# Every fourth split of a weight tile has its lower part subtracted by GpSimd in place of VectorE

## The chip, the core and the metric

The kernel runs on one core of one Trainium2 chip. The metric is the device time of one execution in microseconds, as the median of repeated executions. The core's engines work side by side, each with its own in-order queue: TensorE (PE in the rows, its weight loads PEld) multiplies matrices, VectorE (DVE) and ScalarE (ACT) work elementwise, GpSimd (POOL) here clears a few tiles and issues some DMAs, SyncE (SP) issues the others.

## The reference

One decoder block over 512 tokens of 1024 channels, in float32. The input is normed; its products with `w_in` feed a gated short convolution and a differential attention of 8 heads; both are gated, added and put back into the residual. A cross-attention of 4 heads over 256 memory positions follows. Last, a layer of 16384 single-neuron experts: each of 8 heads scores 2 x 128 keys, keeps the best 16 of each half, then the best 16 of their sums, softmaxes these, and the chosen rows of `peer_u` and `peer_v` give

```python
act = gelu(einsum('td,thkd->thk', hc, peer_u[experts]))
out = einsum('thk,thkd->td', g * act, peer_v[experts])
```

The sum with the residual is normed once more.

## The kernel before

Activations lie channel by token: a product has a weight tile of 1024 x 128 (eight blocks of 128 x 128) on one side and up to 512 tokens on the other.

**The split.** Every float32 product runs as three passes in TensorE's faster float32r format, over exact two-part splits: high x high, high x low, low x high. ScalarE copies the tile `raw` to `hi`, which rounds it; the lower part is what is left, `lo = raw - hi`. `split` (line 97) does both; its second line is an instruction of VectorE over 128 x 1024 float32. `weight` (line 106) loads a tile on SyncE's queue and splits it; `product` (line 114) then issues 8 x 3 matmuls, of which the third already reads `lo`. The tags `raw`, `hi` and `lo` have three buffers each, so a tile is loaded and split while the two before it are multiplied, and `hi` of a new tile waits until the product three tiles back has been done.

**The stages in order of time.** The memory's keys and values (12 tiles by `weight`). The eight heads and the convolution (48 tiles); then the gated outputs, the mix, the cross-attention and its output (56 tiles). The choice of keys, `keys_scores` and `keys_pairs`: 16 tiles of `w_pq`, and VectorE's searches for the best 16. The gates, `gates` (line 823): for blocks of 24 tokens, one-hot rows by ScalarE and VectorE, multiplied by TensorE. During keys and gates TensorE also runs products of `uT`, 96 of 128 tiles by `stage_u` (line 687), to fill its waits. The experts' loop, `experts` (line 713): for each of 128 blocks j it loads a tile of `peer_v`, splits it with the same tags, multiplies the activations by the gates (line 739, VectorE), splits these (`tr` by ScalarE and `e` by VectorE) and adds 18 matmuls of 512 columns to six banks (line 750). For j from 85 to 116 each step also runs one of the other 32 `uT` tiles.

**GpSimd's queue.** In the heads it clears masked blocks of the attention weights (lines 304 and 305), whose buffers come free with the matmuls of line 312. At the start it writes the table of the relative bias to DRAM (line 219). The first 128 tokens take their experts by gathered rows, `gathered` (line 774): one indirect DMA per row (line 818), 256 in all, issued by GpSimd after VectorE has copied the row's index (line 798) and the row's buffer is free (VectorE's lines 801 and 812, whose weight comes by the copy of line 808).

**What sets the order.** The program is written stage by stage, but the order of each engine's queue is laid out by a planner, which simulates the program with its own costs (`schedule_with_timeline_sim`, line 933) and puts the instructions of all engines in the order of that simulated time. On the chip each engine keeps to that order and waits at the head of its queue.

Of the kernel before, what the change touches and what calls it, by code (L numbers as in the profile page):

```python
"""Hybrid block on one core: gated short conv + differential attention, memory cross-attention, PEER.

Activations are channel-major ([channel, token]) up to the expert layer. Every float32 product runs
as three float32r passes over exact two-part splits (hi*hi + hi*lo + lo*hi). The expert layer takes
the first 128 tokens by gathering the rows they chose, and the other 384 against all experts on the
tensor engine, with the gates laid out densely.
"""
# [34 lines left out]
# the order of the work  # L42
EARLY = 5  # convolution channels kept beside the chunks
LAG = 1  # heads before the first convolution channels
SOON = 5  # memory weights loaded ahead of the input
PROLOGUE = 96  # blocks of experts activated before the first is summed up
BY_HEAD = 5  # of them, by each head's choice of experts
BY_BLOCK = 3  # and by each block of tokens' gates
FILL = 4  # and at the end of the gates
AHEAD = 11  # blocks activated ahead of the sum after that  # L50
NA = 3  # one-hot rows of four that ScalarE makes
MM = 1  # gate banks taken from the products
X_HEAD = 4  # gathered rows by two heads' choice
X_BLOCK = 3  # and by each block of tokens' gates
XW = 3  # rows in a step with an activation, to one in a step without
LAST = 2  # steps without rows at the end
LAST_J = 2  # blocks summed up token block by token block at the end
# [4 lines left out]
class Block:  # L62
    # tag: (pool, slots)
# [13 lines left out]
    def __init__(self, nc, tc, pools, psum, dram, a):  # L77
        self.nc, self.tc, self.pools, self.psum, self.dram, self.a = nc, tc, pools, psum, dram, a
        self.count = 0

# [10 lines left out]
    def rows(self, name):  # L91
        """a vector on every partition"""
        src = self.a[name]
        return bass.AP(tensor=src.tensor, offset=src.offset, ap=[[0, P], [1, D]])

# [1 line left out]
    def split(self, hi, lo, src):  # L97
        self.nc.scalar.activation(hi, src, AF.Copy)  # L98
        self.nc.vector.tensor_tensor(out=lo, in0=src, in1=hi.bitcast(F32), op=ALU.subtract)  # L99
# [6 lines left out]
    def weight(self, dram_ap):  # L106
        raw = self.t("raw", [P, KC, P])
        self.nc.sync.dma_start(out=raw, in_=dram_ap)
        hi = self.t("hi", [P, KC, P], F32R)
        lo = self.t("lo", [P, KC, P], F32R)  # L110
        self.split(hi, lo, raw)
        return hi, lo

    def product(self, out, w, x):
        """out[c, t] = sum over d of w[d, c] x[d, t]"""
# [22 lines left out]
    def roots(self, out, acc, n, inv, eps, log=False, bank="tr"):  # L138
        """out[t, i] = 1 / sqrt(inv * sum of squares + eps) of token 128 i + t; acc holds sums by partition"""
# [7 lines left out]
    def inverse_root(self, out, ss, inv, eps, log=False):  # L147
        """1 / sqrt(ss * inv + eps). By log: exp(-log / 2), and a Newton step, where ScalarE holds that table; else three
        Newton steps from the exponent halved in the bits"""
# [16 lines left out]
    def spread(self, r, n, bank="tr"):  # L166
        """the tokens' values along the free dim, on every partition (in PSUM)"""
# [24 lines left out]
    def parameters(self):  # L192
        nc, a, m = self.nc, self.a, self.misc
        nc.vector.tensor_scalar(out=self.g_sub, in0=self.small[:, 56:57], scalar1=1.0 - LAM_INIT, scalar2=None, op0=ALU.mult)
        # lambda = exp(q1.k1) - exp(q2.k2) + init, the same on every partition
# [9 lines left out]
        # relative bias by distance, reversed: entry e stands for distance 511 - e  # L205
# [36 lines left out]
    def diff_head(self, h, x):  # L242
# [4 lines left out]
        # each component's 64 channels on both halves of the partitions: queries as (hi, lo), keys as (hi, hi)  # L247
# [21 lines left out]
        for pair in range(2):  # L269
            # weights of two query blocks, two key blocks to a tile  # L270
            ahi = [self.t("aw", [P, 2, 2 * P], F32R) for _ in range(pair + 1)]
            alo = [self.t("aw", [P, 2, 2 * P], F32R) for _ in range(pair + 1)]
            for qi in range(2):
# [24 lines left out]
                for b in range(pair + 1):  # L298
# [3 lines left out]
                    if m == 1:  # L302
                        # this key block is all in the future of the pair's first query block
# [32 lines left out]
    def gated(self, sg, w_out, y, gate, x):  # L336
        """sigmoid(gate projection) * (y @ w_out)"""
# [7 lines left out]
    def add_and_scale(self, w, y, res, g):  # L345
        """res += y @ w, in place; returns the split of res * g, and the sums of squares by partition"""
# [19 lines left out]
    def memory(self):  # L366
        """keys and values of the cross-attention, to DRAM: the products need no norm, which scales the positions"""
# [5 lines left out]
        # some weights ahead of the input, which the norm needs as a whole  # L373
# [50 lines left out]
    def mem_keys(self):  # L424
        """channel-major: [channel, position] by chunk"""
        out = []
# [7 lines left out]
    def mem_values(self):  # L434
        """token-major: [position, part, position block, channel] by chunk"""
# [62 lines left out]
    def keys_scores(self, h, x, yk, xk):  # L498
        """the best 16 keys of each half, for the dense and for the gathered tokens"""
# [15 lines left out]
    def keys_pairs(self, n, vals, idx, ei, ej, ez):  # L515
        """the best 16 sums of one from each half, for n pairs of a head and a block of tokens: rows, columns, sums less the largest"""
# [5 lines left out]
        # a sum can be among the 16 best only with fewer than 16 pairs before it in both lists: all b for a < 4, b < 4 from there  # L522
# [10 lines left out]
        # place -> (a, b); the places from 64 hold four b for each a from 4  # L533
# [10 lines left out]
        for c, e in ((0, ei), (1, ej)):  # L544
            # small integers, exact in bfloat16; one term of each sum is not zero
# [12 lines left out]
    def keys_gates(self, eg, rtok):  # L558
        """softmax over each head's 16"""
# [15 lines left out]
    def load_x(self, tag):  # L575
        """channel-major, as chunks"""
# [5 lines left out]
    def tokens(self):  # L582
# [4 lines left out]
        with left("att") as self.pools["h"]:  # L587
# [9 lines left out]
            # the convolution's products fill the waits of the attention's chains  # L597
# [35 lines left out]
        # normed channels of the dense tokens  # L633
# [29 lines left out]
    def by_token(self, xT, rtok):  # L663
        """the residual by token, to DRAM until the end; the gathered tokens' normed rows"""
# [18 lines left out]
    def act_tile(self, j):  # L683
        """the two tags take turns, sixteen each"""
        return self.t("BA"[j // 16 % 2], [P, TY])

    def stage_u(self):
        """the dense tokens' activations of the next 128 experts (i, j) of one j; those that find no room wait in DRAM"""
# [24 lines left out]
    def experts(self):  # L713
# [6 lines left out]
        # the gathered rows to each step, by its share of the tensor engine's time  # L720
# [4 lines left out]
        for j in range(NK):  # L725
# [9 lines left out]
            self.split(vh, vl, raw)  # L735
# [7 lines left out]
            if j < NK - LAST_J or j == NK - 1:  # L743
                # the last few together, so that the tokens' blocks end one after the other
# [9 lines left out]
        # residual, final norm  # L754
# [19 lines left out]
    def gathered(self):  # L774
        """the first tokens' experts by gathered rows; a generator that is sent the number of rows for a step"""
# [9 lines left out]
        while True:  # L785
# [6 lines left out]
            # a step's indices and weights; taking its turn with the tiles of that tag, the tile keeps the step to its place  # L792
# [30 lines left out]
    def gates(self, ei, ej, eg):  # L823
        """the dense tokens' gates over all experts, in DRAM: [block of tokens, i, j, token]"""
# [112 lines left out]
```

## Time and profile before

| what | value |
|---|---|
| median of the timed runs | 2159.45 us (2159.32 and 2159.57) |
| profiled execution: span from the first to the last instruction | 2152.3 us, 7.15 us less than the median |
| mean granted TensorE clock | 0.985 of the full 2.4 GHz |
| busy share: TensorE, its weight loads, VectorE, ScalarE, GpSimd | 95%, 82%, 70%, 47%, 16% |
| DMA, mean over the span | 204 GB/s |

The profiled execution's own time is its span; the timed median also holds what lies around it. Busy shares are averages over stages with different limits, so they are read stage by stage. A wait is put down to what ended it. A line of the kernel can be that of a helper: line 99 splits every tile, and the tile's name tells which (`lo<-raw,hi` is a weight tile). Idle time of an engine on which nobody waits costs nothing.

### The profile page before, as it was taken

What the parts mean: (1) busy time and instruction counts of PE and PEld (TensorE: products, weight loads), DVE (VectorE), ACT (ScalarE), POOL (GpSimd) and SP (SyncE); (2) the same over time, 40 slices, a digit from 0 to 9 for tenths busy, and PEclk for the clock granted to TensorE, in tenths of its full rate; (3) what the DMA queues carried; (4) which work ended last, traced back from release to release, by engine and by line L of the source; (5) the groups of instructions that cost most, each with busy time, mean ns of one, the idle gap of its engine ahead of it and who ended that gap; (6) DMA issues with size and microseconds to landing.
All of it is one profiled execution on the core that took longest, in us unless ns stands there. A gap on an engine that the chain in (4) does not pass through costs nothing.

```text
span 2152.3 us, 29167 instructions
## 1 busy us (share of the span) xinstructions
PE 2048.0 (95%) x10341; PEld 1772.6 (82%) x10341; DVE 1505.0 (70%) x3531; ACT 1004.1 (47%) x1716; POOL 341.4 (16%) x301
## 2 busy tenths in 40 slices
PE   7499999999999999999998999999999999999997
PEld 6477877788887878899898989988777877888985
DVE  5356565642345568999887777557887887887897
ACT  5244444432233344343369999953333333333332
POOL 1000000000000000001231111012222234564431
PEclk9799999999999999999999999999999999999999
DMA  7532222223433124246687777589999988899984
GB/s 219 135 98 74 74 85 78 69 88 98 145 110 100 60 78 127 87 129 219 206 281 273 266 279 244 194 299 307 350 321 333 340 310 276 312 357 352 350 298 157
DMA packets 162787, 440.09 MB, mean 204 GB/s; under 512 B 15185, under 2 KB 70497, under 8 KB 160593
## 3 DMA queue, kind: packets, MB, share of 16 engines
q1 hardware_dynamic: 124464, 300.98, 41.7%
q0 software_dynamic: 38176, 137.25, 18.6%
q8 instruction: 81, 1.33, 0.2%
q14 instruction: 66, 0.53, 0.1%
HBM read 391.50 MB, written 46.66 MB: 204 GB/s over the span
## 4 chain that ended last, share of the span: by engine, by line
PE 51%; DMA 13%; DVE 13%; ACT 12%; issue 7%; POOL 2%; another core or an unknown queue 2%; SPq 0%; ACTq 0%; DVEq 0%; POOLq 0%
PE psmm L120 30%; PE psmm L750 5%; ACT slot L858 5%; PE pslg L120 5%; PE pstr L750 4%; DVE lo L99 3%; DMA raw<-in_peer_v 3%; DMA res<-in_peer_v,e 3%; ACT sq L850 3%; DMA act<-sp 2%; ACT hi L98 2%; PE pspv L750 2%; DMA res<-in_peer_u,e 1%; DMA res<-in_peer_u,kp 1%
## 5 line engine op out<-in xcount | busy, mean ns | idle before, releaser
L98 ACT ACTIVATE hi<-raw 128x1024 fp32r<-128x1024 f32 x388 | 410.9, 1061 | 633.0 <-PE psmm L120 288.4
L99 DVE TENSOR_TENSOR lo<-raw,hi 128x1024 fp32r<-128x1024 f32 x388 | 472.7, 1220 | 302.4 <-ACT hi L98 296.1
L120 PE MATMUL psmm<-A,hi 128*128 128x512 f32 x1408 | 451.1, 397 | 1.9 <-DVE Yb L450 1.9
L120 PE MATMUL psmm<-n,hi 128*128 128x384 f32 x1472 | 391.4, 343 | 1.2 <-ACT sp L695 1.2
L120 PEld LDWEIGHTS psmm<-A,hi 128*128 128x128 f32 x1408 | 262.3, 188 | 60.0 <-issue 4.2
L120 PE MATMUL psmm<-A,lo 128*128 128x512 f32 x704 | 280.6, 399 | 0.0
L120 PEld LDWEIGHTS psmm<-n,hi 128*128 128x128 f32 x1472 | 266.7, 188 | 1.6 <-ACT sp L695 1.5
L120 PE MATMUL psmm<-n,lo 128*128 128x384 f32 x736 | 251.6, 342 | 4.7 <-DVE lo L99 4.5
L818 POOL DMA_INDIRECT res<-in_peer_u,e x85 | 94.1, 1107 | 453.9 <-DVE e L798 430.2
L120 PEld LDWEIGHTS psmm<-A,lo 128*128 128x128 f32 x704 | 132.7, 189 | 28.6 <-issue 2.0
L98 ACT ACTIVATE tr<-e 128x384 fp32r<-128x384 f32 x128 | 66.6, 520 | 182.9 <-DVE e L739 179.0
L120 PE MATMUL pslg<-n,hi 128*128 128x384 f32 x576 | 148.3, 338 | 0.0
L120 PEld LDWEIGHTS psmm<-n,lo 128*128 128x128 f32 x736 | 138.3, 188 | 8.2 <-DVE lo L99 7.9
L750 PE MATMUL psmm<-hi,tr 128*128 128x512 f32 x384 | 129.0, 400 | 15.5 <-ACT tr L98 8.5
L801 DVE CUSTOM_DVE_ANT_0 res<-res,hx 128x1024 f32<-128x1024 f32 x101 | 122.5, 1219 | 24.8 <-DMA res<-in_peer_u,e 16.9
L750 PE MATMUL psmm<-lo,tr 128*128 128x512 f32 x384 | 131.1, 396 | 0.3 <-DVE lo L99 0.3
L818 POOL DMA_INDIRECT res<-in_peer_v,e x74 | 103.7, 1401 | 125.2 <-DVE e L808 103.1
L750 PE MATMUL psmm<-hi,e 128*128 128x512 f32 x384 | 119.6, 397 | 1.7 <-DVE e L798 1.6
L818 POOL DMA_INDIRECT res<-in_peer_u,kp x16 | 20.4, 1274 | 616.5 <-DVE kp L798 552.7
L120 PEld LDWEIGHTS pslg<-n,hi 128*128 128x128 f32 x576 | 105.3, 188 | 3.1
L856 DVE TENSOR_SCALAR oh<-iota,e 128x128 f32<-128x128 f32 x384 | 106.8, 345 | 0.0
L812 DVE SCALAR_TENSOR_TENSOR acc<-res,e,acc 128x1024 f32<-128x1024 f32 x73 | 93.5, 1281 | 15.8 <-DMA res<-in_peer_v,e 15.6
(299 smaller groups left out, 3748.2 us busy)
## 6 DMA issues: line engine op xcount, KB each, us to landing
raw<-in_uT SPq DMA_DIRECT2D x128, 512.0 KB, 4.5
raw<-in_peer_v SPq DMA_DIRECT2D x128, 512.0 KB, 5.9
raw<-in_w_in SPq DMA_DIRECT2D x64, 512.0 KB, 3.5
gates<-slot SPq DMA_DIRECT2D x16, 1536.0 KB, 6.7
slot<-gates SPq DMA_DIRECT2D x16, 1536.0 KB, 12.2
act<-sp SPq DMA_DIRECT2D x64, 192.0 KB, 3.8
raw<-in_w_pq SPq DMA_DIRECT2D x16, 512.0 KB, 3.5
raw<-in_w_ckv SPq DMA_DIRECT2D x12, 512.0 KB, 7.5
```

The costliest lines, as they stand in the source:

```text
L98: self.nc.scalar.activation(hi, src, AF.Copy)
L99: self.nc.vector.tensor_tensor(out=lo, in0=src, in1=hi.bitcast(F32), op=ALU.subtract)
L120: self.nc.tensor.matmul(out, ww[:, k, :], xx, start=(k == 0 and p == 0), stop=(k == KC - 1 and p == 2))
L750: nc.tensor.matmul(accs[2 * i + half], l[:, ts], m[:, half * 512 : half * 512 + 512], start=(jj == 0 and p == 0), stop=(jj == NK - 1 and p ...
L801: nc.vector.tensor_tensor_reduce(out=t, in0=t, in1=hx, op0=ALU.mult, op1=ALU.add, scale=1.0, scalar=0.0, accum_out=wx[:, 0, s : s + 1])
L812: nc.vector.scalar_tensor_tensor(out=acc, in0=t, scalar=w, in1=acc, op0=ALU.mult, op1=ALU.add)
L818: nc.gpsimd.indirect_dma_start(out=t, out_offset=None, in_=a["peer_u"] if s < P else a["peer_v"], in_offset=bass.IndirectOffsetOnAxis(ap=i ...
L850: nc.scalar.activation(sq[:, w, :], self.iota, AF.Square, bias=it[:, t0 + w : t0 + w + 1], scale=-1.0)
L856: nc.vector.tensor_scalar(out=oh[:, 4 + w, :], in0=self.iota, scalar1=cols[:, 0, t - b * TB : t - b * TB + 1], scalar2=cols[:, 1, t - b * ...
L858: nc.scalar.copy(stage[:, :, q * 4 : q * 4 + 4].rearrange("p j w -> p w j"), pp.rearrange("p (w j) -> p w j", w=4))
```

## The change

`split` takes the engine that subtracts. A method `turns` counts the tiles and names GpSimd for every fourth and VectorE for the rest. `weight` and the experts' split of `peer_v` pass its answer on; all other splits stay on VectorE. ScalarE's half, the loads, the buffers and the products are as before, and the planner lays the queues out anew. The rest of the diff takes comments out and leaves the line numbers nearly where they were.

```diff
-        self.count = 0
+        self.count = self.tiles = 0
...
-    def split(self, hi, lo, src):
+    def split(self, hi, lo, src, engine=None):
         self.nc.scalar.activation(hi, src, AF.Copy)
-        self.nc.vector.tensor_tensor(out=lo, in0=src, in1=hi.bitcast(F32), op=ALU.subtract)
+        (engine or self.nc.vector).tensor_tensor(out=lo, in0=src, in1=hi.bitcast(F32), op=ALU.subtract)
+
+    def turns(self):
+
+        self.tiles += 1
+        return self.nc.gpsimd if self.tiles % 4 == 0 else self.nc.vector
...
     def weight(self, dram_ap):
...
-        self.split(hi, lo, raw)
+        self.split(hi, lo, raw, self.turns())
         return hi, lo
...
             vh, vl = self.t("hi", [P, D], F32R), self.t("lo", [P, D], F32R)
-            self.split(vh, vl, raw)
+            self.split(vh, vl, raw, self.turns())
```

## Rows read from the trace of the kernel before

**Rows 1.** The page: busy us of each engine (share of span), instructions.

```profile
PE 2048.0 (95%) x10341; PEld 1772.6 (82%) x10341; DVE 1505.0 (70%) x3531; ACT 1004.1 (47%) x1716; POOL 341.4 (16%) x301
```

**Rows 2.** Stages (us from:to): attention, keys, gates, first and last experts.

```profile
core 0: us, PE busy (x) PEld busy (x) DVE busy (x) ACT busy (x) POOL busy (x), PEclk, DMA share, GB/s
...
98.00:455.00 357.00, 357.00 (x1703) 282.92 (x1702) 220.38 (x496) 166.49 (x350) 5.90 (x27) 1.00 0.27 83
...
825.00:1062.00 237.00, 232.98 (x1270) 217.60 (x1269) 227.72 (x959) 88.80 (x126) 25.17 (x19) 1.00 0.48 155
1062.00:1421.00 359.00, 341.50 (x2147) 329.90 (x2146) 260.32 (x704) 325.83 (x602) 49.41 (x45) 1.00 0.72 252
1421.00:1840.00 419.00, 403.07 (x1755) 329.91 (x1754) 314.57 (x551) 145.60 (x194) 116.25 (x96) 0.98 0.92 322
1840.00:2090.00 250.00, 244.35 (x1218) 220.40 (x1217) 216.34 (x330) 86.14 (x117) 129.93 (x89) 1.00 0.94 338
```

**Rows 3.** Waits of TensorE's weight loads, whole span: us in total, times, longest.

```profile
PEld psmm L120 <- ACT hi L98: 38.3, 7, 13.9
...
PEld pstr L857 <- ACT oh L851: 13.6, 26, 1.6
PEld psmm L750 <- ACT tr L98: 13.2, 12, 3.2
...
PEld psmm L120 <- DVE lo L99: 7.9, 10, 1.5
...
PEld pslg L120 <- DVE lo L99: 5.1, 3, 2.0
```

**Rows 4.** The page's costliest groups: busy, mean ns | idle before, releaser.

```profile
L98 ACT ACTIVATE hi<-raw 128x1024 fp32r<-128x1024 f32 x388 | 410.9, 1061 | 633.0 <-PE psmm L120 288.4
L99 DVE TENSOR_TENSOR lo<-raw,hi 128x1024 fp32r<-128x1024 f32 x388 | 472.7, 1220 | 302.4 <-ACT hi L98 296.1
```

**Rows 5.** GpSimd's instructions by line: busy us, mean ns of one.

```profile
L305 POOL MEMSET aw<- 128x128 f32 x16 | 3.8, 240 | 241.3 <-PE pspv L312 241.3
```

**Rows 6.** All waits of the span.

```profile
ACT hi L98 <- PE psmm L120: 288.4, 113, 4.4
```

**Rows 7.** The chain that ended last: start us, us, what.

```profile
1911.72 4.24 PE pslg L120 x24
```

**Rows 8.** GpSimd in order of time: start us, us, and the wait before.

```profile
86.57 0.21 POOL L304 MEMSET aw<- 128x128 f32 x1 [54.87 <-DMA toep<-aw]
150.20 0.41 POOL L305 MEMSET aw<- 128x128 f32 x1 [63.42 <-PE pspv L312]
```

**Rows 9.** Line 99 in keys, gates, first, last experts: ns min/median/max.

```profile
L99 DVE TENSOR_TENSOR lo<-raw,hi x46: 1164/1207/1225, 827.9 to 1058.6; 128x1024 fp32r<-128x1024 f32 x46
...
L99 DVE TENSOR_TENSOR lo<-raw,hi x59: 1209/1224/1237, 1065.6 to 1419.7; 128x1024 fp32r<-128x1024 f32 x59
...
L99 DVE TENSOR_TENSOR lo<-raw,hi x93: 1215/1220/1228, 1424.0 to 1836.1; 128x1024 fp32r<-128x1024 f32 x93
...
L99 DVE TENSOR_TENSOR lo<-raw,hi x59: 1208/1217/1226, 1840.8 to 2085.6; 128x1024 fp32r<-128x1024 f32 x59
```

**Rows 10.** Waits in the gates, 1062 to 1421 us.

```profile
POOL res L818 <- DVE e L798: 202.8, 14, 34.1
```

**Rows 11.** GpSimd's waits in the first experts, 1421 to 1840 us.

```profile
POOL res L818 <- DVE e L798: 234.3, 36, 112.1
...
POOL oh L818 <- DVE e L808: 23.4, 6, 10.0
```

**Rows 12.** GpSimd's waits in the last experts, 1840 to 2090 us.

```profile
POOL oh L818 <- DVE e L808: 44.5, 9, 10.0
POOL res L818 <- DVE e L808: 44.1, 15, 8.0
```

**Rows 13.** All engines in order of time, around 1737 us.

```profile
1736.34 1.27 DVE L812 SCALAR_TENSOR_TENSOR acc<-oh,e,acc 128x1024 f32<-128x1024 f32 x1
1736.63 3.87 POOL L818 DMA_INDIRECT res<-in_peer_v,e  x1 [1.19 <-DVE e L798]
1737.54 0.55 DVE L739 TENSOR_TENSOR e<-B,slot 128x384 f32<-128x384 f32 x1
1738.01 1.22 DVE L99 TENSOR_TENSOR lo<-raw,hi 128x1024 fp32r<-128x1024 f32 x1
...
1740.81 0.94 POOL L818 DMA_INDIRECT res<-in_peer_v,e  x1 [0.30 <-DVE e L739]
```

## The prediction

> **What bounds the kernel.** I read the busy line of the page first: TensorE is busy 95% of the span, VectorE 70%, GpSimd 16% [rows 1]. A share is an average, so the second view is the table by stage [rows 2]. TensorE is full in the attention (357 of 357 us), where VectorE has 38% to spare. In the choice of keys VectorE is the full one: 227.7 of 237 us. In the gates it is ScalarE (325.8 of 359). In the first experts VectorE has a quarter to spare (314.6 of 419), in the last an eighth (216.3 of 250). The third view is what TensorE's weight loads wait for [rows 3]. The tile that this change touches, `lo` of line 99, is waited for 7.9 + 5.1 = 13.0 us in all. The long waits are for `hi` (38.3 us, most of it at the start, where a DMA is late), for ScalarE's one-hot rows (13.6) and for the experts' `tr` (13.2). So TensorE bounds nearly everywhere, and VectorE's subtraction itself holds it up for 0.6% of the span.
>
> **What moves.** Two callers pass the new argument. `weight` is called 12 times for the memory, 64 for the input projections, 8 each for conv_out, attn_out, mix_out, cq and co, 16 for pq and 128 for uT: 260. The loop over the experts splits 128 tiles of peer_v. That makes the 388 subtractions of the trace [rows 4], and every fourth of one running count is 97 on GpSimd. In the last experts uT and peer_v alternate; the count stands at 313 when uT comes back, so the multiples of four fall on every second uT tile, never on peer_v. VectorE loses 97 x 1.22 = 118 us of its 1505.
>
> **What one costs on GpSimd.** No GpSimd arithmetic is in the trace. Lower end: 1.2 us, the same instruction on VectorE [rows 4]. Upper end: GpSimd's memset of 128x128 takes 240 ns [rows 5]; eight make 1.9 us for one stream of 1024 elements, and three streams (two in, one out) 5.8 us. I take 1.9: the same engine, with the memset's fixed part counted eight times to stand for the second input. That is 184 us more for a GpSimd busy 341. The Trainium skill's "GPSIMD Engine Reference", § 3.1, puts a two-input add at about twice VectorE's time; an estimate from it is 2.4 us, or 233 us for 97, with the same sum below.
>
> **Does the lateness show?** ScalarE's `hi` waits 288.4 us, in 113 waits, for the product that last held the buffer [rows 6]. There are three buffers, so a tile is split while two whole products lie ahead of it. A product of 24 matmuls of 384 columns takes 4.24 us [rows 7]. Spare time: 2 x 4.24 - 1.06 (`hi`) - 1.22 (`lo`) = 6.2 us. At 1.9 us on GpSimd 5.5 are left, at 5.8 still 1.6. The longer subtraction by itself costs nothing; those two products hide it, and the projections' have more columns still. What can use the 5.5 us up is the queue: GpSimd works in order, so a subtraction may stand behind a memset or an indirect DMA that waits, and those behind it wait for ScalarE's `hi`.
>
> **The sum, stage by stage.**
> - Start (3 of the 97). A memset stands until 86.57 us behind the write of the bias table, after 54.87 us of waiting [rows 8]. A subtraction behind it comes late, but TensorE already waits there for `hi`, which covers most. 0 to +5 us, taken +1.
> - Attention and projections (98 to 825, 27 moved). The 13.0 us of waits for `lo` lie in the keys (7.9) and the last experts (5.1), so nothing is to be gained here. Memsets wait up to 63.42 us at the head of the queue [rows 8] for the sums of line 312. The planner orders both queues by one simulated time, so a product due before such a sum should keep its subtraction ahead of the memset. 0 to +10, taken +1.
> - Keys (46 tiles [rows 9], 11.5 moved). VectorE loses 11.5 x 1.21 = 14 us where it is full; TensorE returns at most the 7.9 us that it waits for `lo`. 0 to -8, taken -4.
> - Gates (59 tiles, 15 moved). ScalarE bounds, so no gain. The indirect DMAs stand 202.8 us, 14 times, for VectorE's index copy [rows 10]. 0 to +42 (second rival), taken +3.
> - First experts (93 tiles, 23 moved). VectorE loses 28 us of 314.6. TensorE's 13.2 us for `tr`, which ScalarE makes from a VectorE product, could shrink; against it one row is issued per step behind an index copy, with 234.3 us of waits of which one of 112.1 is the stage's beginning, and 10.0 us the longest other [rows 11]. (234.3 - 112.1) / 35 = 3.5 us on average is inside the 5.5. -13 to +20, taken +1.
> - Last experts (59 tiles, 15 moved). Gain at most the 5.1 us of waits for `lo`. The queue's head waits 44.5 + 44.1 us, 3.7 on average, at most 10.0 [rows 12]; three rows per step now share GpSimd with the subtractions. If all 15 met the longest, 15 x 4.5 = +67; the mean fits. -5 to +67, taken +5.
> - End (2 or 3). On GpSimd the last tile no longer stands behind VectorE's final adds, and runs longer: 0.
>
> Sum: 1 + 1 - 4 + 3 + 1 + 5 = +7. The profiled execution spans 2152.3 us, and the timed median of 2159.45 lies 7.15 above it, which I leave. 2152.3 + 7 + 7.15 = **2166 us**: no change that can be told (2%, 43 us, is about what a measurement of this kernel can tell from no change).
>
> **Rivals.**
> - *VectorE is held while GpSimd reads.* For: one DMA issue on GpSimd takes 3.87 us, its neighbour 0.94, and the long one lies beside VectorE's two-input instructions back to back [rows 13]. Against: VectorE's own instruction never exceeds 1.24 us [rows 9], though nothing on GpSimd reads a tile now. Price: each moved subtraction takes 1.9 us from VectorE in place of 1.22. It counts where VectorE is full: 11.5 x (1.9 - 1.21) = +8 in the keys in place of -4, so **2178**. At 5.8 us each the keys pay 11.5 x 4.6 = +53 and the last experts 15 x 4.6 - 34 to spare = +35, so 2166 + 4 + 88 = 2258. The Trainium skill's "SBUF — State Buffer", § Who interferes with whom, states such a lock between a VectorE instruction with two SBUF inputs and a GpSimd instruction that reads SBUF: the later one waits for the whole of the other. By that rule this rival holds; no row here has both sides.
> - *GpSimd's queue jams (slower).* Place: the gates. The head is blocked 202.8 us in 14 waits, 14.5 each. A subtraction that falls at random into one stands 0 to 14.5 us, and beyond 5.5 TensorE waits: (14.5 - 5.5)^2 / (2 x 14.5) = 2.8 us on average. All 15: +42 in place of +3, **2205**. For: these waits cover 56% of that stage. Against: the planner puts a subtraction behind the DMAs only where it expects those first. It decides once the queue holds a subtraction longer than 5.5 us.
> - *VectorE was the hidden bound (faster).* The 13.0 us for `lo` and the 13.2 for `tr` go and nothing comes: 2159 - 26 = **2133**. Against: three of four subtractions stay.
> - *The change does nothing:* all is hidden, the planner orders as before, 2159, inside the forecast's own 2150 to 2180.
>
> **Chances.** Forecast 0.55 (with the last rival), held VectorE 0.22, jam 0.13, faster 0.10. The range of 8 in 10, 2142 to 2212, leaves out most of the faster case, a quarter of the held one (a subtraction nearer 5.8 than 1.9) and a third of the jam: 0.07 + 0.055 + 0.045 = 0.17. Above 2202.6 lie half of the jam (0.065), 0.3 of the held case (0.066) and 0.02 for an order that no row shows: 0.15. Below 2116 a gain of 43 us would need more than all the waits named: 0.02. Within: 0.83.
>
> **What would show it.** Right: 97 subtractions on GpSimd near 2 us, VectorE's busy time down some 118 us, fewer waits for VectorE's `lo` in the keys, a few us of waits for GpSimd's `lo` in gates and experts. The held VectorE would show as two-input instructions far above 1.24 us; the jam as weight loads that wait for GpSimd in the gates, some 3 us each. The prediction is wrong if a subtraction takes over 5.8 us, so that two products no longer cover it, or if TensorE comes to wait in the attention.

## The result, and the profile after

The changed kernel takes 2217.59 us (2217.01 to 2218.16) where the kernel before takes 2159.45: **1.0269 times as long, interval 1.0239 to 1.0298, slower by 58 us**. The prediction was 2166 us, its range 2142 to 2212. In the text below lines have the numbers of the changed kernel, which lie five above those of before from line 105 on (matmuls of the gates 862 for 857, of the experts 755 for 750, gate product 744 for 739). Rows of another run have that run's own line numbers.

The profiled execution spans 2215.2 us against 2152.3, so 62.9 us are to be found (63.0 before rounding, as in the table of the experiments). The busy line of the changed kernel's page, which answers to [rows 1]:

```profile
PE 2068.5 (93%) x10341; PEld 1786.7 (81%) x10341; DVE 1541.5 (70%) x3434; ACT 999.9 (45%) x1716; POOL 597.3 (27%) x398
```

VectorE has 97 instructions fewer and yet is busy 36.5 us longer. The 97 subtractions would have taken 97 x 1.22 = 118 us there, so its other instructions have grown by 155 us, 1.6 us for each tile moved. TensorE runs the same 10341 matmuls in 20.5 us more, and its idle time grows by 62.9 - 20.5 = 42.4 us.

The table by stage, boundaries moved to where the stages now lie, answers to [rows 2]:

```profile
core 0: us, PE busy (x) PEld busy (x) DVE busy (x) ACT busy (x) POOL busy (x), PEclk, DMA share, GB/s
98.00:455.00 357.00, 357.00 (x1695) 282.44 (x1694) 222.49 (x482) 164.66 (x350) 36.12 (x44) 1.00 0.28 84
825.00:1070.00 245.00, 233.48 (x1251) 218.91 (x1249) 237.83 (x963) 86.84 (x123) 63.82 (x31) 0.98 0.46 149
1070.00:1434.00 364.00, 343.50 (x2152) 335.50 (x2151) 257.49 (x675) 324.31 (x601) 89.90 (x59) 0.98 0.72 249
1450.00:1863.00 413.00, 383.61 (x1604) 304.90 (x1605) 307.37 (x494) 132.83 (x181) 159.99 (x106) 0.97 0.84 293
1863.00:2146.00 283.00, 268.41 (x1305) 240.67 (x1305) 242.99 (x338) 92.72 (x126) 178.47 (x113) 0.97 0.92 328
```

The attention is as full as before and loses nothing. In the fourth row, the sums of the first 85 blocks, TensorE does 1604 matmuls in 413 us with 29 us of idle time. The same piece of the kernel before:

```profile
1434.00:1816.00 382.00, 371.42 (x1599) 301.71 (x1600) 296.05 (x520) 135.70 (x182) 106.14 (x89) 0.99 0.92 321
```

Here the idle time is 11 us. VectorE has 26 instructions fewer after the change and is busy 11 us longer; the transfers fall from 321 to 293 GB/s.

**What a moved tile does.** All engines of the changed kernel in order of time (start us, us, engine, line):

```profile
1636.81 2.55 POOL L99 TENSOR_TENSOR lo<-raw,hi 128x1024 fp32r<-128x1024 f32 x1
...
1637.04 2.74 DVE L99 TENSOR_TENSOR e<-e,tr 128x384 fp32r<-128x384 f32 x1
...
1639.82 0.56 DVE L744 TENSOR_TENSOR e<-B,slot 128x384 f32<-128x384 f32 x1
...
1640.47 0.53 ACT L98 ACTIVATE tr<-e 128x384 fp32r<-128x384 f32 x1 [3.93 <-DVE e L744]
```

While GpSimd subtracts, a VectorE instruction with two SBUF inputs that takes 0.55 us elsewhere takes 2.74 and ends 0.42 us after GpSimd's. All 19 such `e` that the trace has above 1.2 us beside a subtraction end 0.41 to 0.43 us after it: the held one goes through when GpSimd is done. The product queued behind it starts 2.2 us late, and ScalarE's `tr` with it. In this place TensorE still has matmuls queued and loses nothing; a hold costs only where it runs out of them. Durations in the kernel before (ns min/median/max), by line:

```profile
L99 DVE TENSOR_TENSOR e<-e,tr x128: 544/552/589, 1433.2 to 2131.1; 128x384 fp32r<-128x384 f32 x128
...
L856 DVE TENSOR_SCALAR oh<-iota,e x384: 327/341/549, 1101.9 to 1413.4; 128x128 f32<-128x128 f32 x192
```

And in the changed kernel:

```profile
L99 DVE TENSOR_TENSOR lo<-raw,hi x291: 1196/1221/3410, 6.4 to 2191.2; 128x1024 fp32r<-128x1024 f32 x146
...
L99 DVE TENSOR_TENSOR e<-e,tr x128: 541/553/2764, 1446.0 to 2195.7; 128x384 fp32r<-128x384 f32 x128
L99 POOL TENSOR_TENSOR lo<-raw,hi x97: 2336/2408/6189, 28.0 to 2191.8; 128x1024 fp32r<-128x1024 f32 x97
...
L861 DVE TENSOR_SCALAR oh<-iota,e x384: 328/342/3024, 1108.5 to 1423.5; 128x128 f32<-128x128 f32 x192
```

The medians stand, the maxima grow by 2.2 us and more: `lo` was never above 1.237 us [rows 9]. So it is a wait for another instruction, not a slower engine.

The Trainium skill's "SBUF — State Buffer", § Who interferes with whom, states this for two SBUF inputs beside a GpSimd instruction that reads SBUF, and for `copy` and `tensor_scalar` in their two-port modes; the 3.02 us of line 861, a `tensor_scalar`, agrees, if it runs in such a mode, which no row shows.

**Who waits.** Waits of the changed kernel over the whole span (us, times, longest), beside [rows 3]:

```profile
POOL lo L99 <- ACT hi L98: 912.4, 55, 37.9
ACT tr L98 <- DVE e L744: 283.7, 101, 8.5
...
PEld psmm L755 <- ACT tr L98: 23.6, 17, 4.8
...
PEld psmm L125 <- DVE lo L99: 13.5, 9, 3.5
...
PEld psmm L755 <- DVE e L99: 12.2, 11, 2.9
...
PEld pslg L125 <- POOL lo L99: 3.8, 3, 2.8
PEld psmm L125 <- POOL lo L99: 3.7, 2, 3.4
...
PEld psmm L755 <- POOL lo L99: 2.4, 1, 2.4
```

TensorE's waits for VectorE's results and for `tr`, which hangs on them, grow; its waits for GpSimd's own `lo` are 9.9 us in all. A second change stands in SyncE's queue, where the loads of the weight tiles wait for a free `raw` buffer. Before, whole span:

```profile
SPq L108 <- DVE lo L99: 709.1, 170, 31.2
...
SPq L733 <- DVE lo L99: 232.9, 102, 6.7
```

After:

```profile
SPq L113 <- DVE lo L99: 573.8, 145, 32.3
SPq L738 <- DVE lo L99: 175.8, 75, 9.2
SPq L113 <- POOL lo L99: 133.0, 33, 9.2
SPq L738 <- POOL lo L99: 122.4, 29, 6.8
```

`raw` has three buffers, and the subtraction is its last reader. Already before the change 272 of the 388 loads waited for it, 942 us in all; after it the waits for either engine's `lo` are 1005 us. GpSimd is a later last reader. These waits alone don't say that `raw` is scarce, for a queue that runs ahead waits for a free buffer in any case. Which of the two ways costs what, the trace can't say; the runs below say it for the first and in part for the second.

### The profile page after: what moved, and what is told of

The parts are those of the page before. It is cut to its first block, busy times and chain, and to the rows that moved or that the text cites. A ratio compares the mean times of both kernels' runs of the same rounds, so it can differ in the third digit from the quotient of the medians.

```text
span 2215.2 us, 29221 instructions
## 1 busy us (share of the span) xinstructions
PE 2068.5 (93%) x10341; PEld 1786.7 (81%) x10341; DVE 1541.5 (70%) x3434; ACT 999.9 (45%) x1716; POOL 597.3 (27%) x398
## 4 chain that ended last, share of the span: by engine, by line
PE 43%; DMA 18%; DVE 16%; issue 9%; ACT 8%; POOL 5%; SPq 1%; DVEq 0%; ACTq 0%; POOLq 0%
PE psmm L125 32%; DMA res<-in_peer_v,e 3%; DMA raw<-in_peer_v 3%; DVE lo L99 3%; DMA res<-in_peer_u,e 3%; ACT slot L863 3%; POOL res L823 3%; DMA raw<-in_w_ckv 2%; PE psmm L755 2%; PE pslg L125 2%; ACT sq L855 2%; DMA oh<-in_peer_v,e 2%; DVE e L99 2%; DVE acc L817 1%; POOL lo L99 1%
## 5 line engine op out<-in xcount | busy, mean ns | idle before, releaser
L99 POOL TENSOR_TENSOR lo<-raw,hi 128x1024 fp32r<-128x1024 f32 x97 | 250.4, 2581 | 1067.4 <-ACT hi L98 912.4
L99 DVE TENSOR_TENSOR lo<-raw,hi 128x1024 fp32r<-128x1024 f32 x291 | 363.3, 1249 | 201.1 <-ACT hi L98 199.2
L125 PE MATMUL psmm<-n,hi 128*128 128x384 f32 x1472 | 396.2, 348 | 5.7 <-ACT sp L700 4.3
L125 PEld LDWEIGHTS psmm<-n,hi 128*128 128x128 f32 x1472 | 271.9, 192 | 6.6 <-ACT sp L700 4.9
L823 POOL DMA_INDIRECT res<-in_peer_u,e x85 | 107.0, 1258 | 228.2 <-DVE e L803 197.2
L806 DVE CUSTOM_DVE_ANT_0 res<-res,hx 128x1024 f32<-128x1024 f32 x101 | 132.3, 1314 | 45.7 <-DMA res<-in_peer_u,e 39.9
L755 PE MATMUL psmm<-hi,e 128*128 128x512 f32 x384 | 126.3, 403 | 9.5 <-DVE e L803 6.9
L99 DVE TENSOR_TENSOR e<-e,tr 128x384 fp32r<-128x384 f32 x128 | 110.6, 864 | 24.9 <-ACT tr L98 23.3
L861 DVE TENSOR_SCALAR oh<-iota,e 128x128 f32<-128x128 f32 x384 | 120.1, 390 | 0.0
L755 PEld LDWEIGHTS psmm<-hi,tr 128*128 128x128 f32 x384 | 71.8, 192 | 49.0 <-ACT tr L98 23.6
```

The lines of the kernel that those rows point to most:

```text
L99: (engine or self.nc.vector).tensor_tensor(out=lo, in0=src, in1=hi.bitcast(F32), op=ALU.subtract)
L125: self.nc.tensor.matmul(out, ww[:, k, :], xx, start=(k == 0 and p == 0), stop=(k == KC - 1 and p == 2))
L755: nc.tensor.matmul(accs[2 * i + half], l[:, ts], m[:, half * 512 : half * 512 + 512], start=(jj == 0 and p == 0), stop=(jj == NK - 1 and p ...
L806: nc.vector.tensor_tensor_reduce(out=t, in0=t, in1=hx, op0=ALU.mult, op1=ALU.add, scale=1.0, scalar=0.0, accum_out=wx[:, 0, s : s + 1])
L823: nc.gpsimd.indirect_dma_start(out=t, out_offset=None, in_=a["peer_u"] if s < P else a["peer_v"], in_offset=bass.IndirectOffsetOnAxis(ap=i ...
L861: nc.vector.tensor_scalar(out=oh[:, 4 + w, :], in0=self.iota, scalar1=cols[:, 0, t - b * TB : t - b * TB + 1], scalar2=cols[:, 1, t - b * ...
```

## The experiments

All ran beside the kernel before. "Later" is against the profiled execution of before, at four marks: the first matmul of the gates (1102.3 us before), of the experts' sums (1434.2), of the 86th block's sum, which ends the sums of the first 85 (1816.6), and the end (2152.3). Single executions differ at these marks by some 5 us, and by up to 7 at the third, with no subtraction moved: e12 lies 6.5 early there and e3 5.7. The end varies more: the 25 timed executions of the kernel before beside e1 to e4 span 2144.8 to 2164.4 us. So the ratio says whether a kernel is slower, and the marks say roughly where.

| kernel | ratio, interval | TensorE busy | gates | sums | 86th | end |
|---|---|---|---|---|---|---|
| before | 1 | 2048.0 | 0 | 0 | 0 | 0 |
| changed | 1.0269 (1.0239 to 1.0298) | 2068.5 | +7.3 | +16.3 | +46.0 | +63.0 |
| e1 lower part left out | 0.9992 (0.9969 to 1.0015) | 2045.2 | -11.9 | +3.1 | +2.6 | +3.3 |
| e2 GpSimd reads besides | 1.0450 (1.0401 to 1.0499) | 2071.7 | +7.7 | +31.7 | +61.7 | +103.8 |
| e3 GpSimd writes besides | 1.0051 (1.0030 to 1.0071) | 2048.7 | -1.7 | -0.2 | -5.7 | +1.4 |
| e4 peer_v alone | 1.0058 (1.0036 to 1.0080) | 2050.1 | -1.4 | +0.4 | +12.7 | +11.4 |
| e5 weight() alone | 1.0193 (1.0156 to 1.0230) | 2065.7 | +6.7 | +20.4 | +36.4 | +51.3 |
| e6 first 116 tiles alone | 0.9981 (0.9961 to 1.0000) | 2051.4 | +0.2 | +4.6 | +4.5 | +2.4 |
| e7 changed, rows later | 1.0276 (1.0238 to 1.0314) | 2062.6 | +8.4 | +19.3 | +36.1 | +56.6 |
| e8 every eighth | 1.0180 (1.0144 to 1.0216) | 2058.3 | +1.1 | +14.5 | +31.4 | +44.6 |
| e9 GpSimd only writes | 0.9975 (0.9952 to 0.9998) | 2046.3 | -10.6 | -4.6 | -1.1 | +0.1 |
| e10 the same, weight() alone | 1.0022 (1.0001 to 1.0044) | 2045.4 | -10.1 | -4.1 | +7.9 | +5.4 |
| e11 e5, rows later | 1.0241 (1.0184 to 1.0298) | 2059.6 | +7.3 | +21.0 | +35.2 | +54.3 |
| e12 before, rows later | 1.0011 (0.9992 to 1.0030) | 2045.6 | 0.0 | +4.2 | -6.5 | +0.7 |
| e13 GpSimd reads hi alone | 1.0156 (1.0139 to 1.0173) | 2056.9 | +2.1 | +14.3 | +21.0 | +37.7 |
| e14 raw given back later | 1.0079 (1.0049 to 1.0110) | 2053.2 | -0.2 | +6.8 | +7.0 | +16.4 |

**Reading, or the queue and the order?**

e1: products of a tile whose turn it is use `hi` in place of `lo`; nobody subtracts.

```diff
+        if self.turns() is self.nc.gpsimd:
+            self.nc.scalar.activation(hi, raw, AF.Copy)
+            return hi, hi
...
+            if self.turns() is self.nc.gpsimd:
+                nc.scalar.activation(vh, raw, AF.Copy)
+                vl = vh
```

> Every fourth lower part is not computed by any engine; the products of those tiles read the upper part in its place, so the number of matmuls is the same and the output is not the reference's. VectorE is as light as in the changed kernel (118 us less), the planner lays its queue out for that, and GpSimd subtracts nothing. Held VectorE (GpSimd's reading stops VectorE's two-input instructions): no reading, so 2140 to 2160 us. New order (the planner's queues for a lighter VectorE put the gathered rows' use too close to their DMAs): 2190 to 2220. Late rows (indirect DMAs stand behind subtractions): 2140 to 2160.

The time stays (2154.67 us). A planner's order for a VectorE that is lighter by these 97 subtractions doesn't by itself cost anything.

e2 and e3 let VectorE make all 388 lower parts, and GpSimd writes `lo` of every fourth tile first: once with an instruction that reads `raw`, once with one that reads nothing.

```diff
 def split(self, hi, lo, src, engine=None):
+        if engine is self.nc.gpsimd:
+            engine.tensor_tensor(out=lo, in0=src, in1=src, op=ALU.subtract)   # e2
+            engine.memset(lo.bitcast(F32), 0.0)                               # e3
         self.nc.scalar.activation(hi, src, AF.Copy)
-        (engine or self.nc.vector).tensor_tensor(out=lo, in0=src, in1=hi.bitcast(F32), op=ALU.subtract)
+        self.nc.vector.tensor_tensor(out=lo, in0=src, in1=hi.bitcast(F32), op=ALU.subtract)
```

> VectorE makes all 388 lower parts, as before. For every fourth tile GpSimd first writes raw - raw into the same lo buffer, and VectorE then writes the true value over it. Held VectorE: VectorE loses about 1.6 us per tile and is not relieved, so at least the changed kernel's time, 2215 to 2260 us. New order: VectorE is as full as before, 2155 to 2175. Late rows: GpSimd is as busy but does not wait for ScalarE's copy, 2165 to 2195.

> As the run with raw - raw, but GpSimd only clears the lo buffer (it writes 128x1024 and reads nothing) before VectorE makes all 388 lower parts. Held VectorE: nothing is read, so VectorE's instructions keep 1.22 us; 2157 to 2172 us. New order: 2155 to 2175. Late rows: GpSimd is occupied about 1 to 2 us per tile instead of 2.4, so 2162 to 2185.

Groups of e2 (busy, mean ns | idle before), then of e3:

```profile
L101 DVE TENSOR_TENSOR lo<-raw,hi 128x1024 fp32r<-128x1024 f32 x388 | 491.8, 1270 | 243.6 <-ACT hi L100 184.1 <-POOL lo L99 50.7 <-PE psmm L127 4.2
L99 POOL TENSOR_TENSOR lo<-raw 128x1024 fp32r<-128x1024 f32 x97 | 198.1, 2042 | 1110.4 <-PE psmm L127 808.6 <-DMA raw<-in_w_ckv 63.2 <-DMA raw<-in_peer_v 47.2
```

```profile
L101 DVE TENSOR_TENSOR lo<-raw,hi 128x1024 fp32r<-128x1024 f32 x388 | 473.0, 1221 | 294.1 <-ACT hi L100 225.8 <-POOL lo L99 51.0 <-issue 10.0
L99 POOL MEMSET lo<- 128x1024 f32 x97 | 93.9, 968 | 1119.7 <-PE psmm L127 1015.2 <-PE pspv L757 40.0 <-DVE xki L500 26.7
```

In both VectorE's `lo` waits some 51 us for GpSimd, so that wait is not the difference. The run that reads costs 4.5% and stretches VectorE's mean `lo` from 1221 to 1270 ns; the one that writes costs 0.5%, with an interval clear of 1, and leaves that mean alone (the +1.4 us in the table is from the fastest of its ten executions). Writing took half as long, which e9 mends: there GpSimd clears `lo` of the moved tiles twice and VectorE does not subtract them.

```diff
+        if engine is self.nc.gpsimd:
+            for _ in range(2):
+                engine.memset(lo.bitcast(F32), 0.0)
+            return
...
```

> Leaves out the lower part of the 97 moved tiles: GpSimd clears the tile twice (about 1.9 us) in place of the subtraction, so GpSimd is occupied about as in the changed kernel and the order is near its order, but GpSimd reads nothing. If GpSimd's reading holds VectorE and that is the loss: before 0 to +8 us (2155 to 2163), VectorE's busy time down some 118 us, no VectorE instruction stretched. If the occupied queue of GpSimd (index copies, row DMAs behind it) is the loss: +40 us or more, as in the changed kernel.

194 clears of 967 ns occupy GpSimd for 187 us, and the time is that of before, if anything 0.25% less. e1 and e9 differ by GpSimd's occupation, and it costs nothing. VectorE's two-input instructions in e9, by line; the changed kernel's longest are 3410 and 2764 ns:

```profile
L103 DVE TENSOR_TENSOR lo<-raw,hi x291: 1162/1224/1264, 6.5 to 2127.4; 128x1024 fp32r<-128x1024 f32 x146
L103 DVE TENSOR_TENSOR e<-e,tr x128: 539/554/591, 1423.6 to 2130.8; 128x384 fp32r<-128x384 f32 x128
```

My expectation that no instruction is stretched was right for those with two inputs alone: the one-input `tensor_scalar` of the one-hot rows takes up to 1748 ns in e9, and 157 us in all against 132 before (549 ns at most).

```profile
L865 DVE TENSOR_SCALAR oh<-iota,e x384: 328/343/1748, 1089.4 to 1402.8; 128x128 f32<-128x128 f32 x192
```

That lies in the gates, where ScalarE bounds, and e9 loses nothing by it. So neither GpSimd's occupation nor the new order is the cause, with two reservations. A clear doesn't wait for ScalarE's `hi`, as the subtraction does. And in e1 and e9 nothing reads `raw` of a moved tile behind ScalarE, so it is given back earlier than in the kernel before, which may hide a small cost. SyncE's waits for `raw` in e9:

```profile
SPq L117 <- DVE lo L103: 618.7, 139, 10.7
SPq L117 <- ACT hi L98: 183.6, 44, 28.7
...
SPq L742 <- DVE lo L103: 163.9, 71, 6.2
...
SPq L742 <- ACT hi L98: 48.9, 28, 6.1
```

They are 1015 us, more than the 942 of before and the 1005 of the changed kernel, and e9 loses nothing: the length of these waits is no measure of harm. e1 and e9 also show what VectorE's 118 us are worth when nothing is paid for them: 12 and 11 us at the first gate and nothing at the end. In e1 the gates give them back, in e9 the gates and the first experts.

**Held VectorE, or `raw` given back late?** e9 takes both away. e13 has GpSimd subtract `hi` from `hi`, which still reads SBUF but lets go of `raw` as soon as ScalarE has read it, as e9 does; e14 has VectorE make every `lo`, and GpSimd then clears the used `raw` of every fourth tile twice, which reads nothing but keeps the buffer.

```diff
+        if engine is self.nc.gpsimd:      # e13
+            src = hi.bitcast(F32)
         (engine or self.nc.vector).tensor_tensor(out=lo, in0=src, in1=hi.bitcast(F32), op=ALU.subtract)
...
+        if engine is self.nc.gpsimd:      # e14, behind VectorE's subtraction
+            for _ in range(2):
+                engine.memset(src, 0.0)
```

> The changed kernel, but GpSimd subtracts hi from hi (leaves out the lower part of the 97 moved tiles): the same instruction, length and wait for ScalarE, yet raw is given back to the next load as soon as ScalarE has read it. The run that clears the tile instead (2150) differs by the reading alone. Held VectorE: +50 to +65 us as in the changed kernel (2205 to 2220). If loads that wait for GpSimd to give raw back (SyncE's queue stands 42 us for that in the first experts of the changed kernel) are the loss: near 2150 to 2160. Both: in between.

> VectorE makes all 388 lower parts; then GpSimd clears the used raw tile of every fourth twice (some 1.9 us), which reads nothing but keeps raw from the next load that much longer, more than the changed kernel's 1.2 us. If late loads are part of the loss: +10 to +30 us (2165 to 2185), most of it in the experts. If only the reading matters: -2 to +5 us (2153 to 2160).

e13, durations by line; then e14, SyncE's waits and a duration:

```profile
L101 DVE TENSOR_TENSOR e<-e,tr x128: 544/551/2566, 1443.7 to 2170.3; 128x384 fp32r<-128x384 f32 x128
...
L101 POOL TENSOR_TENSOR lo<-hi x97: 1882/1900/6714, 28.3 to 2165.6; 128x1024 fp32r<-128x1024 f32 x97
```

```profile
SPq L116 <- POOL raw L102: 243.0, 46, 11.0
...
SPq L741 <- POOL raw L102: 140.2, 27, 9.6
```

```profile
L99 DVE TENSOR_TENSOR e<-e,tr x128: 544/552/592, 1440.0 to 2149.0; 128x384 fp32r<-128x384 f32 x128
```

The reading alone costs: e13 loses 1.6% where e9, which gives `raw` back at the same moment and occupies GpSimd for nearly as long, loses nothing. e13's reading and its wait for ScalarE's `hi` are what is left between them, and e2, whose GpSimd doesn't wait for `hi`, loses 4.5%. That the held VectorE is the larger part of the loss is shown.

Of `raw` given back late less is shown. e14 loses 0.8% though no two-input instruction is held there (`e` at most 592 ns). But GpSimd's clears also hold its one-hot `tensor_scalar`s, by 29 us in the gates, and e3, where VectorE is as full and the clears half as long, loses 0.5%, with an interval that overlaps e14's. The 9.4 us that e14 loses between the third mark and the end settle nothing: e3 and e12 lose 7.1 and 7.2 there. So late `raw` alone costs at most about these 0.8% (interval 0.5 to 1.1), and how much of them is open.

I had expected "in between" for e13 if both held, and that is what came. e13 and e14 together make 2.4%, the change 2.7%, which agrees within the intervals. But e13's instruction is shorter than the real one (mean 2094 against 2581 ns), and part of the missing 1.1% may be that length: an estimate by it is 1.6% x 2581 / 2094 = 1.9%. And e14 keeps `raw` longer (1.9 us of clears behind VectorE's subtraction, against some 1.4 us more for GpSimd's). By stage the two don't add up: between the second and third mark they lose 6.7 and 0.2 us where the change loses 30, behind the third 16.7 and 9.4 where it loses 17. Why is not settled.

**Where a moved tile costs.** e4 and e5 move one kind of tile alone, e6 only the first 116 (29 moved), e8 every eighth.

```diff
-            self.split(vh, vl, raw, self.turns())           # e5: peer_v stays with VectorE
+            self.turns()
+            self.split(vh, vl, raw)
...
-        return self.nc.gpsimd if self.tiles % 4 == 0 else self.nc.vector
+        return self.nc.gpsimd if self.tiles % 4 == 0 and self.tiles <= 116 else self.nc.vector   # e6
+        return self.nc.gpsimd if self.tiles % 8 == 0 else self.nc.vector                         # e8
```

> The same count, but only peer_v's tiles pass the engine on: 24 to 32 subtractions on GpSimd, none before the experts. In the changed kernel the stretch up to the first expert lost 16 us, the experts 45. Held VectorE: the experts' loss stays for the most part, 2185 to 2200 us, and the time up to the first expert is that of before. New order: the same, if the order inside the experts is what costs; 2165 to 2200. If the loss in the experts came from the stages before it, 2160.

> The running count and its order are those of the changed kernel, but a peer_v tile whose turn it is stays with VectorE; only the tiles of weight() pass to GpSimd (73 of 97). In the first experts only what is left of weight() is moved there (next to nothing). If the loss there is the hold of VectorE by each moved tile, that stage costs as before (382 us) and the whole is before +63 - 30 = +33 (2187 to 2195). If the loss there is what the earlier stages hand over (rows and gates late), that stage stays some 20 us longer or more and the whole is at +50 or more. If the two kinds of tiles add up, this and the run with peer_v alone (+11) make 63, so this one would be at +50.

> GpSimd subtracts only among the first 116 tiles (29 of 97: the attention and the projections), VectorE all behind them. Held VectorE, with price only where VectorE's results are waited for: before -1 to +3 us (2155 to 2163), though the 29 moved tiles hold VectorE some 45 us. A hold that costs the same everywhere: 29/97 of 63 = +19 us (2178).

> Every eighth tile and not every fourth goes to GpSimd (48 of 97). A price for each moved tile: half the loss, +31 us (2186 to 2195). If VectorE's time to spare takes up the first holds and only those beyond it count, well under half: +5 to +20 us. A cost of the queue's new order alone: no fixed relation, up to the full +63.

e4 took 2167 us and not the 2185 to 2200 that I had expected of a held VectorE: the 24 moved tiles of `peer_v` are not most of the experts' loss. e4 and e5 together make 1.0251, the change itself 1.0269: the two kinds add up, the third case of e5's expectation. e6 is free: 29 moved tiles cost nothing where TensorE has products queued and VectorE has time to spare (38% in the attention). No kernel here that does the whole work is faster than the kernel before by what a run can tell; e6 (0.9981, its interval ending at 1) is the nearest. e8 moves half as many tiles and loses two thirds of the time (1.8% of 2.7%), where I had expected half or less. Why the first moved tiles cost more than those between them was not tried.

**Rows that have not landed.** e5 loses 16 us between second and third mark with no moved tile there, and VectorE's waits for gathered rows had grown. e7, e11 and e12 use a row two steps after its issue and not one, in the changed kernel, in e5 and in the kernel before; e10 is e5 with clears in place of the subtractions.

```diff
-            for k, (s, t) in enumerate(pend):
+            wait = []
+            if len(rows) > 4:
+                wait = [x for x in pend if x[2] == 1]
+                pend = [x for x in pend if x[2] != 1]
+            for k, (s, t, _) in enumerate(pend):
...
-            pend = []
+            pend = [(s, t, 0) for s, t, _ in wait]
...
-                pend.append((s, t))
+                pend.append((s, t, 1 if len(rows) > 4 else 0))
```

> The changed kernel, with the gathered rows of a step used two steps after their issue and not one. If the first experts lose 30 us and not the 12 of the run with peer_v alone because VectorE comes to rows that have not landed (its waits for row DMAs are 40 us against 17), some 13 to 18 us come back there: 2198 to 2205. If all of it is the hold itself, the time stays within 5 us of the changed kernel (2213 to 2222), or is longer.

> As the run before it, but for the tiles of weight() alone (73); VectorE makes all of peer_v's lower parts. In the run with real subtractions there (+44 to +51) the first experts lost 16 us without one moved tile among them. If that is the order (rows used closer behind their issue, with VectorE fully loaded): the first experts lose 12 to 16 us here too, the whole +10 to +20 (2165 to 2175). If it was handed over by the held VectorE of the gates: nothing is lost there, the whole -5 to +5.

> Only weight() tiles move to GpSimd (73), and a gathered row is used two steps after its issue and not one. If the 16 us that the first experts lost without a moved tile are waits for rows that have not landed: they come back, whole +28 to +38 us (2183 to 2193) against the +44 without this edit. If not: +44 to +50.

> The kernel before with rows used two steps after their issue, the rest untouched: the baseline of the run before it, and the one candidate here for a faster kernel. VectorE's waits for row DMAs are 17 to 27 us in all there and it has a quarter to spare: -4 to +2 us (2151 to 2157) by every theory; more than -5 would say that rows in flight bounded the kernel before, too; more than +5 that the edit has a price of its own in the last experts.

My idea failed: e7 and e11 bring nothing back (1.0276 for 1.0269; 1.0241 for 1.0193, above both ranges that I had named). e10 also loses 12 us in that piece, but starts it 4 us early and ends 5 us late in all, below the +10 to +20 that I had tied to those 12. So e5's 16 us there may partly be this order's way of spreading its time, and the runs don't divide them further.

## Why the prediction was wrong

**The step that failed** is the choice between the forecast and its first rival, and then that rival's price. Every term of the sum took VectorE to be 118 us lighter; it is 36.5 us busier. The rival, "VectorE is held while GpSimd reads", is what the runs show (e9 against e13); it stood at 0.22 because VectorE's own instruction never exceeds 1.24 us [rows 9]. That row says nothing of a GpSimd that reads, as the prediction itself noted, and should have carried no weight. The rival was then priced only "where VectorE is full", and as the difference of two durations, 1.9 - 1.21 us. For the keys that came close: +8 predicted, +8.8 measured from the first uT product (907.2 before, 905.7 after) to the first gate. With no reading (e9) the same piece gains 4.6, the forecast's own -4. Some of that is luck: the price took the whole of a 1.9 us subtraction from VectorE, while the subtraction takes 2.58 us and VectorE's other instructions grow by 1.6 us for each. And a hold is not a quantity of work that spare time swallows. It lands on one instruction, here 2.2 us on `e`, with the gate product, `tr` and the index copy queued behind it. An average of a quarter to spare didn't cover that: the first experts lost 29.7 us where the rival, too, had +1.

**"The longer subtraction by itself costs nothing"** was half right. The two products ahead do cover it for the reader of `lo`: TensorE waits 9.9 us in all for GpSimd's `lo`, and e9 shows that the queue costs nothing. But a subtraction has a second customer, the next load into `raw`. The 6.2 us to spare were reckoned from a `raw` that is there, and the prediction gave its later return no term. e14 bounds that at some 0.8%; how much of it is the late `raw` stays open.

**GpSimd's price** was taken as 1.9 us, inside bounds of 1.2 to 5.8; it is 2.34 to 2.41 in half of the cases and 2.58 on average. The Trainium skill's "GPSIMD Engine Reference", § 3.1, from which the estimate 2.4 was worked out, agrees with that median. This term was too small by a quarter to a third and changed no sign.

**The jam** did not come: weight loads wait for GpSimd's `lo` 9.9 us over the whole span, where it had them wait 42 in the gates. **The hidden bound** is refuted by e1: with the 97 subtractions gone altogether the time stays.

**By stage**, predicted against measured: start, attention and projections +2, measured -1.5; keys -4, +8.8; gates +3, +9; first experts +1, +29.7; last experts +5, +10.5; end 0, +6.5. The gates' +9 should not be read closely: e6 and e12, with nothing moved there, show +4.

## Part of the loss is TensorE's clock

The prediction had no term for it. TensorE's busy time rises by 20.5 us with the same matmuls, a third of the profiled loss, and in e2, e5, e8 and e13 by 24, 18, 10 and 9, kernels in which TensorE stalls more; in e3, e9 and e12 by 0.7 at most, in e6, which loses nothing, by 3.4. One stall in the changed kernel shows what follows one. A load of `raw` lands late, TensorE stops, and starts again slowly (start us, us, engine, line):

```profile
1678.37 6.28 SPq L715 DMA_DIRECT2D B<-act  x1
...
1685.22 0.85 SPq L738 DMA_DIRECT2D raw<-in_peer_v  x2
...
1695.69 1.06 ACT L98 ACTIVATE hi<-raw 128x1024 fp32r<-128x1024 f32 x1 [8.69 <-DMA raw<-in_peer_v]
1696.65 0.51 ACT L98 ACTIVATE tr<-e 128x384 fp32r<-128x384 f32 x1
...
1697.21 0.73 PE L755 MATMUL psmm<-hi,tr 128*128 128x512 f32 x2 [4.34 <-ACT tr L98]
```

TensorE alone in the stretches around it (us, busy, matmuls, granted clock, DMA share, GB/s):

```profile
1684.00:1692.50 8.50, 8.50 (x39) 1.00 1.04 390
1692.90:1697.20 4.30, 0.00 (x0) 1.00 0.64 250
1697.20:1701.20 4.00, 3.99 (x11) 0.59 0.28 79
1701.40:1705.00 3.60, 3.60 (x17) 1.00 0.89 289
```

After 4.3 us without a matmul the granted clock is 0.59 over the next 4.0 us, most of it at 1.2 GHz and not 2.4: 11 matmuls where 4.0 us at full clock hold 18 (39 in 8.5). A stall of 4.3 us thus costs 7 x 0.22 = 1.5 us more. Over the whole span the mean granted clock falls from 0.985 to 0.972; 1.3% of 2048 us is 27 us, an estimate near the 20.5. The share is not fixed: the other timed execution of the changed kernel was granted 0.978 and took 1.2 us longer.

What made this load late is not shown to be the change. It was issued behind a load of activations whose issue alone took 6.28 us, and such issues of up to 5 us stand at the same line in the kernel before, where TensorE's longest stall among the first 85 sums is 2.8 us.

## What to carry to other kernels

Work given to GpSimd is not off VectorE if it reads SBUF: look at what VectorE does meanwhile, and price the hold on the instruction that it hits and the chain behind it, not on VectorE's average. When an instruction moves to a slower engine, ask not only who waits for its result but whose buffer it is the last to read. How long the load queue waits for that buffer doesn't answer it (e9 waits longer than the changed kernel and loses nothing); a run that only keeps the buffer longer, like e14, bounds it. And where every freed microsecond of an engine is shown to be worth nothing (e1), there is no upside to set against such risks.

## What the runs showed that I had not expected

- What GpSimd does to SBUF decides which VectorE instructions it holds. Its writes (clears of 128x1024, e9) left `lo` at 1264 ns at most and `e` at 591, but held the one-input `tensor_scalar` of 128x128 up to 1748 ns, against 549 before; its subtraction held both kinds.
- Small instructions are held as long as large ones: a copy of 128x3 integers took up to 2385 ns in the changed kernel and 170 before. The copies of 128x1 were never held (158 ns at most).
- GpSimd is stretched too: its longest subtraction (6.19 us) stands beside 13 VectorE instructions back to back, 11 of them with two inputs.
- GpSimd's subtraction with one tile as both operands took 1.90 us at the median (e13), with two tiles 2.41.
